# Turning the memory keys of four sequences on VectorE instead of TensorE

## The chip, the cores and the metric

One core of a Trainium2 chip runs the whole program in one launch. The metric is device time in microseconds (us), from the profiler's record of whole runs; a run is a little longer than its span, which goes from the first to the last instruction. TensorE (PE) multiplies matrices, and its weight loads (PEld) are recorded apart; VectorE (DVE) and ScalarE (ACT) work on rows of up to 128 partitions; GpSimd (POOL) does small work; SyncE (SP) issues most DMAs. Each engine runs its own instructions strictly in the order of the program and waits for semaphores of the others.

## The reference, cut to what matters

The program is one step of one decoder layer with width 1024. A prompt of 512 rows and a sample group of 8 sequences of 4 rows each go through the same weights: a mixer, cross-attention and a gated FFN. The change lies in the cross-attention, for the sample group:

```
def mem_attend(h, mk, mv, w_mq, w_mo):
    B, T, _ = h.shape
    q = (h @ w_mq).reshape(B, T, MEM_HEADS, MEM_HEAD_DIM)
    s = jnp.einsum('bqhd,bkhd->bhqk', q, mk) * (MEM_HEAD_DIM ** -0.5)
    p = jax.nn.softmax(s, axis=-1)
    o = jnp.einsum('bhqk,bkhd->bqhd', p, mv).reshape(B, T, D_MODEL)
    return o @ w_mo
```

There are 4 heads of 256. The prompt has one memory of 256 tokens. Each of the 8 sample sequences has 256 memory keys of its own, `cache_mem_k[b]` of 256 x 1024 in float32. The scores sum over the key's 256 head elements. In DRAM and in the SBUF stage the tokens lie on the partitions. A matmul sums over partitions, so the keys have to be turned before they can be an operand.

## The kernel before, in words

Weights and caches come by DMA into the pool `stg`: six stage buffers of 128 x 1024 float32. Weights are split into two fp32r halves (`split`, L146 on ACT and L147 on DVE) and go to the pool `wp`, four slots of 128 x 2 x 1024.

The query projection `h @ w_mq` is a `gemmB` (L465 and L477). Its output goes to `qh` and `ql` (high and low half for the prompt, L1348 and L1349) and to `qs` (the sample's queries, L1351). After it comes the attention, written as two interleaved parts.

The prompt's part is `prompt = pipe(8, ch_soft, idle, ch_turn, ch_out)`. One `next(prompt)` is one step: `ch_out` of item t-3, `ch_turn` of item t-2, `ch_soft` of item t, in that order. An item is one head with 256 rows. `ch_soft` has 12 score matmuls into `sca` (L1367), a maximum `cnm` on DVE (L1370), two exponentials on ACT (L1373), a reciprocal (L1374) and two scalings on DVE that write `cp` (L1376). `ch_turn` has four PE transposes into `cpt` (L1385), split into `pT` by ACT and DVE. `ch_out` has matmuls into `cpo` (L1397), split into `oT` by ACT and DVE.

The sample's part works on 16 chunks, two for each sequence, of 128 tokens x 1024. `mk_load` (L1407) brings a chunk into a stage buffer. `mk_turn` transposes it with eight PE transposes into `tpk` (L1416) in two groups of four, and each group is copied from PSUM to `kT`, in a slot of `wp` (L1417; the first group by ACT, the second by DVE). `mk_scores` (L1424) makes a sequence's scores `ssc` with eight matmuls, one for each head and half of its 256 elements; four of them lie side by side in TensorE's columns. Then come a maximum `snm` on DVE (L1035) and an exponential on ACT (L1036). Chunks 0 to 7 are turned during the query gemm; chunks 8 to 15, those of sequences 4 to 7, stand between the prompt's first steps. The values are then loaded by `mv_load` (L1428 and L1436) and summed in `mv_out` into `pso` (L1446).

What sets the order: the engines' programs are ordered by a scheduler from the order of the source; `tc.issue_after(x)` keeps what is written inside it behind instruction x, and `tc.high_priority()` moves work ahead. PSUM has two pools: five buffers (`mmp`: sca, ssc, cpo, pso and others) and three (`at`: tpk, cpt and others). Behind the attention stands the gemm with `w_mo`, and before it 24 small DMAs on SP's queue bring the convolution's rows into the tile `cr` (L1511 to L1513), which PE transposes later (`cvp`, L1525).

Of the kernel before, what the change touches and what calls it, by code (L numbers as in the profile page):

```python
# [7 lines left out]
F32 = mybir.dt.float32  # L8
F32R = mybir.dt.float32r
BF16 = mybir.dt.bfloat16  # L10
I32 = mybir.dt.int32
AF = mybir.ActivationFunctionType
ALU = mybir.AluOpType
AX = mybir.AxisListType

P = 128
DM = 1024
SEQ = 512
NB = 8
TS = 4  # L20
NS = NB * TS
ROWS = SEQ + NS
H = 4
# [54 lines left out]
def kernel(ctx: ExitStack, tc: tile.TileContext, I, O):  # L78
    nc = tc.nc
    MUL, ADD, SUB, MAX, MIN = ALU.mult, ALU.add, ALU.subtract, ALU.max, ALU.min  # L80
    NSLOT = 4
# [7 lines left out]

    cst = ctx.enter_context(tc.tile_pool(name="cst", bufs=1))  # L90
    sp = ctx.enter_context(tc.tile_pool(name="sp", bufs=11))
    wp = ctx.enter_context(tc.tile_pool(name="wp", bufs=NSLOT))
    stg = ctx.enter_context(tc.tile_pool(name="stg", bufs=6))
    npool = ctx.enter_context(tc.tile_pool(name="npool", bufs=5))
    t2p = ctx.enter_context(tc.tile_pool(name="t2p", bufs=8))
    zp = ctx.enter_context(tc.tile_pool(name="zp", bufs=3))
    sm = ctx.enter_context(tc.tile_pool(name="sm", bufs=4))
    psm = ctx.enter_context(tc.tile_pool(name="psm", bufs=5, space=bass.MemoryType.PSUM))
    psa = ctx.enter_context(tc.tile_pool(name="psa", bufs=3, space=bass.MemoryType.PSUM))
    dram = ctx.enter_context(tc.tile_pool(name="dram", bufs=1, space=bass.MemoryType.DRAM))  # L100

    def S(shape, dt, name):
        return sp.tile(list(shape), dt, name=name, tag="S")

    def N(name, w=1024):
        return npool.tile([P, 1032], F32, name=name, tag="N")[:, :w]
# [10 lines left out]
    def mmp(name="mm"):  # L117
        return psm.tile([P, 512], F32, name=name, tag="mm")
# [11 lines left out]
    mm = nc.tensor.matmul  # L130
# [4 lines left out]
    VRED = nc.vector.tensor_reduce  # L135
    VCP = nc.vector.tensor_copy
    GTT = nc.gpsimd.tensor_tensor
    ACT = nc.scalar.activation
    dma = nc.sync.dma_start
# [67 lines left out]
    W = Weights(NSLOT)  # L207
# [2 lines left out]
        return stg.tile([P, 1024], F32, name="wst", tag="st")  # L210

    def slot_tile():
        return wp.tile([P, 2, 1024], F32R, name="wslot", tag="W")

    def split_w(sv, st, share):

# [123 lines left out]
    @contextmanager  # L340
    def burst(ins):

        if ins is None:
            yield
        else:
            with tc.issue_after(ins), tc.high_priority():
                yield
# [227 lines left out]
    for i, _ in enumerate(mem_k()):  # L575
        if i in HSTEPS:
            j = HSTEPS.index(i)
# [53 lines left out]
    kT = S([P, H, ROWS], F32, "kT")  # L631
# [22 lines left out]
    for c0, c1 in HALF:  # L654
        n = c1 - c0
        ps = mmp()
# [3 lines left out]
        t = T2([64, n], "gt")  # L660
# [47 lines left out]
    ps = at("gtp")  # L708
# [3 lines left out]
    ps = at("gtp")  # L712
# [190 lines left out]
    ps = at("npt")  # L903
# [37 lines left out]
    ps = at("nT0")  # L941
# [34 lines left out]
    ps = at("nTt")  # L976
# [17 lines left out]
    r, ss = gq[:, 14:15], gq[:, 15:16]  # L994
# [177 lines left out]
    for b in range(4):  # L1172
        c = slice(b * P, b * P + P)
# [3 lines left out]
    kst, kts, pts, aTs, outs, rcs = {}, {}, {}, {}, {}, {}  # L1177
# [5 lines left out]
            gather("cache_dk", b, g, kst[b][g])  # L1183

    def dk_turn(b):
        kt = kts[b] = wp.tile([P, H, 260], F32, name="kT", tag="W")
        nc.gpsimd.tensor_copy(out=kt[:, :, 256:260], in_=dkT[:, :, SEQ + TS * b:SEQ + TS * (b + 1)])
        for g in range(2):
            ps = at("tpk")
            for h in range(H):  # L1190
                tr(ps[:, h * P:(h + 1) * P], kst[b][g][:, h * P:(h + 1) * P], ident)
            (VCP if g else nc.scalar.copy)(out=kt[:, :, g * P:(g + 1) * P], in_=v2(ps, P))
# [56 lines left out]
    prompt = pipe(4 * H, da_soft, lambda i: None, da_turn, da_av, da_end)  # L1249
    sall = S([P, NB, 260], F32, "das")  # L1250
# [85 lines left out]
    qs = sm.tile([P, 8, NS], F32, name="qs", tag="qz", bufs=1)  # L1336
    qh, ql = [], []

    def ev_q(m):
        if m % 2 == 0:  # L1340
            qh.append(npool.tile([P, 2, 516], F32R, name="qh", tag="N"))
        if m % 4 == 0:
            ql.append(S([P, 4, SEQ], F32R, "ql"))

        def ev(i, c0, c1, ps):
            n = min(c1, SEQ) - c0
            q = qh[m // 2][:, m % 2, c0:c0 + n]
            nc.scalar.mul(out=q, in_=ps[:, :n], mul=1.0 / 16.0)  # L1348
            STT(out=ql[m // 4][:, m % 4, c0:c0 + n], in0=ps[:, :n], scalar=1.0 / 16.0, in1=f32(q), op0=MUL, op1=SUB)  # L1349
            if i == 1:  # L1350
                nc.scalar.mul(out=qs[:, m, :], in_=ps[:, n:n + NS], mul=1.0 / 16.0)  # L1351
        return ev
# [3 lines left out]

    pTs, cps = {}, {}

    def ch_soft(i):
        h, bp = i // 2, i % 2  # L1360
        sv = v2(mmp("sca"), 256)
        for j in range(2):
            t0 = (2 * bp + j) * P
            for c in range(2):
                q, l = qh[h][:, c, t0:t0 + P], ql[h // 2][:, 2 * (h % 2) + c, t0:t0 + P]
                for m, (x, k) in enumerate(((q, 0), (q, 1), (l, 0))):
                    mm(sv[:, j, :], lhsT=x, rhs=mkT[k][:, 2 * h + c, :], start=(c + m == 0), stop=(c == 1 and m == 2))  # L1367
        nm = small(2, "cnm")
        su = small(2, "csu")
        VRED(out=nm, in_=sv, axis=AX.X, op=MAX, negate=True)  # L1370
        p = cps[i] = v2(Z("cp"), 256)
        for j in range(2):
            ACT(out=p[:, j, :], in_=sv[:, j, :], func=AF.Exp, bias=nm[:, j:j + 1], accum_out=su[:, j:j + 1])  # L1373
        nc.vector.reciprocal(out=su, in_=su)  # L1374
        for j in range(2):
            VTS(out=p[:, j, :], in0=p[:, j, :], scalar1=su[:, j:j + 1], scalar2=None, op0=MUL)  # L1376
# [27 lines left out]
    def mk_load(i):  # L1404
        b, c = i // 2, i % 2
        kst[i] = stage()
        dma(out=kst[i], in_=I["cache_mem_k"][0, b, c * P:(c + 1) * P].rearrange("t h d -> t (h d)"))  # L1407

    def mk_turn(i):
        b, c = i // 2, i % 2  # L1410
        if c == 0:
            kts[b] = wp.tile([P, 8, 256], F32, name="kT", tag="W")
        for q in range(2):
            ps = at("tpk")
            for j in range(4):
                t = tr(ps[:, j * P:(j + 1) * P], kst[i][:, (4 * q + j) * P:(4 * q + j + 1) * P], ident)  # L1416
            (VCP if q else nc.scalar.copy)(out=kts[b][:, 4 * q:4 * q + 4, c * P:(c + 1) * P], in_=v2(ps, P))  # L1417
        return t.ins

    def mk_scores(b):  # L1420
        ps = mmp("ssc")[:, :256]
        for c in range(2):
            for h in range(H):
                t = mm(ps[NS * h:NS * h + NS], lhsT=qs[:, 2 * h + c], rhs=kts[b][:, 2 * h + c, :], start=(c == 0), stop=(c == 1))  # L1424
        sample_exp(sall, b, ps, nm, su)
        return t.ins

    def mv_load(b):  # L1428

        if 2 < b < 7:  # L1430
            t = wp.tile([P, 2, DM], F32, name="vt", tag="W")
            vts[b] = [t[:, 0], t[:, 1]]
        else:
            vts[b] = [stage(), stage()]
        for c in range(2):
            dma(out=vts[b][c], in_=I["cache_mem_v"][0, b, c * P:(c + 1) * P].rearrange("t h d -> t (h d)"))  # L1436
# [18 lines left out]
    for i, _ in enumerate(gemmB(hqT, [ev_q(m) for m in range(4, 8)])):  # L1455
        if i % 4 == 3:
            for j in (i // 2 - 1, i // 2):
                mk_turn(j)
                mk_load(j + 6)

    next(prompt)
    for b in range(4):
        t = mk_scores(b)
    with tc.issue_after(t):
        for j in range(8, 16):
            t = mk_turn(j)
            if j + 6 < 2 * NB:
                mk_load(j + 6)
            if j == 11:
                next(prompt)  # L1470
    for b in range(3):
        mv_load(b)
    next(prompt)
    with tc.issue_after(t):
        for b in range(4, NB):
            t = mk_scores(b)
    for b in range(3, 7):
        mv_load(b)
    next(prompt)
# [24 lines left out]

    NUT = 43
    cvT = S([P, NUT, 20], F32, "cvT")
    conv0 = I["state_conv"][0].rearrange("b j c -> (b j) c")

    def conv_in(t, p0, o, c0, n):

        dma(out=t[p0:p0 + 16, o:o + n], in_=conv0[:, c0:c0 + n])  # L1511
        dma(out=t[p0 + 16:p0 + 19, o:o + n], in_=I["w_dw"][0][:, c0:c0 + n])
        dma(out=t[p0 + 19:p0 + 20, o:o + n], in_=I["b_dw"][:, c0:c0 + n])  # L1513


    cr = N("cr")
    for g in range(6):
        conv_in(cr, 20 * g, 0, 896 * g + (64 if g > 2 else 0), 896)
    conv_in(cr, 0, 896, 2688, 64)
    conv_in(cr, 0, 960, 5440, 64)  # L1520
    for t0 in (0, 4):
        ps = at("cvp")
        nt = min(4, 7 - t0)
# [356 lines left out]
```

## Time and profile before

| what | value |
|---|---|
| median of 3 runs | 957.77 us (955.96 to 959.61) |
| the profiled execution | 956.79 us |
| its span | 955.0 us |
| PE busy | 932.7 us, 98% of the span |
| DVE busy | 599.2 us, 63% |
| ACT busy | 388.8 us, 41% |
| mean granted TensorE clock | 0.993 |

The attention of the sample and the prompt lies between 441 and 500 us of the span. A view by lines gives, for each group, the line, the engine, the tiles (out<-in), the shapes, the count, the busy time, the mean duration of one in ns, and after the second bar the idle time before it with what ended it. Matmuls overlap, so a mean duration of theirs is longer than the distance from one start to the next.

### The profile page before, as it was taken

What the parts mean: (1) busy time and instruction counts of PE and PEld (TensorE: products, weight loads), DVE (VectorE), ACT (ScalarE), POOL (GpSimd) and SP (SyncE); (2) the same over time, 40 slices, a digit from 0 to 9 for tenths busy, and PEclk for the clock granted to TensorE, in tenths of its full rate; (3) what the DMA queues carried; (4) which work ended last, traced back from release to release, by engine and by line L of the source; (5) the groups of instructions that cost most, each with busy time, mean ns of one, the idle gap of its engine ahead of it and who ended that gap; (6) DMA issues with size and microseconds to landing.
All of it is one profiled execution on the core that took longest, in us unless ns stands there. A gap on an engine that the chain in (4) does not pass through costs nothing. (4 is left out here: it accounts for less than half of the span.)

```text
span 955.0 us, 17088 instructions
## 1 busy us (share of the span) xinstructions
PE 932.7 (98%) x6619; PEld 810.6 (85%) x6619; DVE 599.2 (63%) x1129; ACT 388.8 (41%) x750; POOL 197.5 (21%) x383
## 2 busy tenths in 40 slices
PE   8999999999999999999999999999999999999995
PEld 5899777879866778998777799989988997999974
DVE  5745144565887448635654769727758676676867
ACT  5655133344676447624544523332212222222232
POOL 6610000024432217300000444001110110111114
PEclk9999999999999999999999999999999999999998
DMA  8950023334825429955953743063053302512023
GB/s 278 309 184 2 1 89 136 89 110 150 264 90 183 155 94 329 307 155 167 353 213 114 206 134 89 4 177 89 4 144 79 122 26 79 165 48 89 24 92 116
DMA packets 120674, 130.27 MB, mean 136 GB/s; under 512 B 8568, under 2 KB 86233, under 8 KB 120593
## 3 DMA queue, kind: packets, MB, share of 16 engines
q1 hardware_dynamic: 114408, 125.69, 41.9%
q10 hardware_dynamic: 6184, 3.48, 1.2%
q8 instruction: 52, 0.85, 0.4%
q14 instruction: 30, 0.24, 0.1%
HBM read 112.22 MB, written 16.93 MB: 135 GB/s over the span
## 5 line engine op out<-in xcount | busy, mean ns | idle before, releaser
L146 ACT CAST wslot<-wst 128x1024 fp32r<-128x1024 f32 x125 | 130.9, 1050 | 259.9 <-issue 74.7
L477 PE MATMUL mm<-fT,wslot 128*128 128x256 f32 x1872 | 235.9, 288 | 0.0
L477 PEld LDWEIGHTS mm<-fT,wslot 128*128 128x128 f32 x1872 | 234.4, 188 | 1.8 <-issue 0.8
L147 DVE TENSOR_TENSOR wslot<-wst,wslot 128x1024 fp32r<-128x1024 f32 x125 | 155.1, 1245 | 89.3 <-ACT wslot L146 88.8
L1691 PE MATMUL mm<-wslot,act 128*128 128x512 f32 (+1 forms) x180 | 70.2, 391 | 0.0
L1692 PE MATMUL mm<-wslot,act 128*128 128x512 f32 (+1 forms) x180 | 70.0, 392 | 0.0
L1690 PE MATMUL mm<-wslot,act 128*128 128x512 f32 (+1 forms) x180 | 69.3, 387 | 0.0
L1598 POOL COPY cvo<-u 128x2 f32<-128x2 f32 x43 | 11.0, 256 | 204.8 <-DVE u L1596 194.7
L407 PE MATMUL mm<-wslot,hT 128*128 128x512 f32 x128 | 52.2, 408 | 0.0
L409 PE MATMUL mm<-wslot,hT 128*128 128x512 f32 x128 | 51.5, 403 | 0.0
L408 PE MATMUL mm<-wslot,hT 128*128 128x512 f32 x128 | 51.3, 401 | 0.0
L477 PE MATMUL mm<-hT,wslot 128*128 128x256 f32 (+1 forms) x384 | 51.0, 289 | 0.0
L1593 DVE TENSOR_TENSOR u<-mm,rsb 128x256 f32<-128x256 f32 x43 | 18.2, 424 | 51.0 <-PE mm L477 50.1
L477 PEld LDWEIGHTS mm<-hT,wslot 128*128 128x128 f32 x384 | 49.2, 188 | 0.5 <-issue 0.2
L1690 PEld LDWEIGHTS mm<-wslot,act 128*128 128x128 f32 x180 | 34.3, 191 | 8.0 <-issue 0.8
L1691 PEld LDWEIGHTS mm<-wslot,act 128*128 128x128 f32 x180 | 33.8, 188 | 7.2
L1692 PEld LDWEIGHTS mm<-wslot,act 128*128 128x128 f32 x180 | 33.8, 188 | 7.2 <-issue 0.4
L1610 ACT ACTIVATE c<-c 128x560 f32<-128x560 f32 x21 | 14.1, 672 | 56.7 <-DVE c L1604 56.7
L1604 DVE SCALAR_TENSOR_TENSOR c<-u,cvT,c 128x560 f32<-128x560 f32 x43 | 34.3, 798 | 0.9
L1603 DVE SCALAR_TENSOR_TENSOR c<-u,cvT,c 128x560 f32<-128x560 f32 x43 | 34.1, 793 | 0.2
L1703 DVE TENSOR_TENSOR yp<-mm,yp 128x512 f32<-128x512 f32 (+1 forms) x41 | 27.2, 674 | 5.1 <-PE mm L1692 5.0
L409 PEld LDWEIGHTS mm<-wslot,hT 128*128 128x128 f32 x128 | 24.5, 191 | 5.3
(474 smaller groups left out, 1857.7 us busy)
## 6 DMA issues: line engine op xcount, KB each, us to landing
wst<-in_w_up_dram SPq DMA_DIRECT2D x42, 512.0 KB
wst<-in_w_in_dram SPq DMA_DIRECT2D x28, 512.0 KB
wst<-in_w_down_dram SPq DMA_DIRECT2D x20, 512.0 KB
wst<-in_cache_mem_k_dram SPq DMA_DIRECT2D x16, 512.0 KB
wst<-in_w_mk_dram SPq DMA_DIRECT2D x8, 512.0 KB
xb<-in_x_prompt_dram SPq DMA_DIRECT2D x8, 512.0 KB
wst<-in_cache_dk_dram SPq DMA_DIRECT2D x16, 256.0 KB
wst<-in_cache_dv_dram SPq DMA_DIRECT2D x16, 256.0 KB
```

Of the source, the lines that this page charges most:

```text
L146: nc.scalar.copy(out=hi, in_=src)
L147: (eng or nc.vector).tensor_tensor(out=lo, in0=src, in1=f32(hi), op=SUB)
L407: mm(ps[b], lhsT=xt.hi(k, c0, c0 + n), rhs=s[:, 0, kk, :], start=(k == 0), stop=False)
L408: mm(ps[b], lhsT=xt.hi(k, c0, c0 + n), rhs=s[:, 1, kk, :], start=False, stop=False)
L409: return mm(ps[b], lhsT=xt.lo(k, c0, c0 + n), rhs=s[:, 0, kk, :], start=False, stop=(k == nk - 1))
L477: mm(ps[i], lhsT=s[:, l, k, :], rhs=x(k, c0, c1), start=(k == 0 and j == 0), stop=(k == 7 and j == 2))
L1603: STT(out=c, in0=u[:, 1:EXT - 1], scalar=w[1], in1=c, op0=MUL, op1=ADD)
L1604: STT(out=c, in0=u[:, 0:EXT - 2], scalar=w[0], in1=c, op0=MUL, op1=ADD)
L1690: mm(ps, lhsT=t[:, 0, c0:c0 + P], rhs=s[:, 0, i % 2, cs], start=st, stop=False)
L1691: mm(ps, lhsT=t[:, 0, c0:c0 + P], rhs=s[:, 1, i % 2, cs], start=False, stop=False)
L1692: return mm(ps, lhsT=t[:, 1, c0:c0 + P], rhs=s[:, 0, i % 2, cs], start=False, stop=en)
L1703: VTT(out=y, in0=ps, in1=y, op=ADD)
```

## The change

The keys of sequences 4 to 7 are no longer turned by PE. VectorE's stream transpose turns 32 x 32 blocks of a chunk from the stage buffer straight into one SBUF tile `kq` of 128 x 4 x 2 x 1024, one instruction per chunk and eight in all. The tile takes the place of the four weight slots: their pool is closed after the scores of sequence 3, the pool of `kq` is opened there, and the weight slots are opened again after the scores of sequences 4 to 7. The eight instructions stand in pairs between the prompt's steps, each held behind the latest `cnm` by `issue_after`.

With 32 x 32 blocks a key's elements lie on 32 partitions, so the scores (`kq_scores`) are 128 matmuls with 32 rows and 32 columns each, in 16 tiles of the array, into four PSUM tiles `ssq`. For the other operand the queries `qs` are written to DRAM (`qs_d`) and read back in four DMAs into `qrep`, where each group of 32 partitions has what it needs. Four copies (two on ACT, two on DVE) bring `ssq` into the order of tokens; one maximum on DVE and four exponentials on ACT follow.

The 24 DMAs of `cr` move from SP's queue to ACT's, into the query gemm.

```
-            kts[b] = wp.tile([P, 8, 256], F32, name="kT", tag="W")
+            kts[b] = slot([P, 8, 256], F32, "kT")
...
+    def kq_turn(i):
+        nc.vector.transpose(kq[:, i // 2 - 4, i % 2], kst[i])
+
+    def kq_scores(t):
+        ps = [mmp("ssq") for _ in range(4)]
+        kt = kq.rearrange("p b c (j r) -> p (b c) j r", r=NS)
+        for j in range(8):
+            for i in range(4):
+                r = slice(NS * i, NS * i + NS)
+                for h in range(H):
+                    with burst(t):
+                        t = mm(ps[i][NS * h:NS * h + NS, :256], lhsT=qrep[r, 2 * h + j // 4, j % 4, :], rhs=kt[r, :, 8 * h + j, :],
+                               start=(j == 0), stop=(j == 7)).ins
+        for i in range(4):
+            (VCP if i % 2 else nc.scalar.copy)(out=sall[:, 4:8, :].rearrange("p b (c i r) -> p b c i r", c=2, i=4)[:, :, :, i, :],
+                                               in_=ps[i][:, :256].rearrange("p (b c r) -> p b c r", c=2, r=NS))
+        VRED(out=nm[:, 4:8], in_=sall[:, 4:8, :], axis=AX.X, op=MAX, negate=True)
+        for b in range(4, 8):
+            ACT(out=sall[:, b, :], in_=sall[:, b, :], func=AF.Exp, bias=nm[:, b:b + 1], accum_out=su[:, b:b + 1])
...
+            conv_rows(i // 2 - 1)
+            conv_rows(i // 2)
 
     next(prompt)
     for b in range(4):
-        t = mk_scores(b)
-    with tc.issue_after(t):
-        for j in range(8, 16):
-            t = mk_turn(j)
-            if j + 6 < 2 * NB:
-                mk_load(j + 6)
-            if j == 11:
-                next(prompt)
+        with tc.issue_after(t):
+            mk_scores(b)
+    for key in list(lay)[::-1]:
+        closed(key)
+    opened("k", 1)
+    kq = lay["k"][1].tile([P, 4, 2, DM], F32, name="kq", tag="K")
+    dma(out=qs_d, in_=qs)
+    for j in range(8, 16):
+        with tc.issue_after(dve_last[0]):
+            kq_turn(j)
+        if j < 10:
+            mk_load(j + 6)
+        if j == 10:
+            for i in range(4):
+                dma(out=qrep[NS * i:NS * i + NS], in_=qs_d.rearrange("(j q) m n -> q m j n", q=NS))
+        if j in (9, 11, 13):
+            next(prompt)
     for b in range(3):
         mv_load(b)
     next(prompt)
-    with tc.issue_after(t):
-        for b in range(4, NB):
-            t = mk_scores(b)
+    kq_scores(pe_last[0])
+    closed("k")
+    opened("w", NSLOT)
+    slots_in("w")
```

VectorE's program before, from the scaling of the prompt's first item to that of its second (`kT<-tpk` are the copies of turned chunks):

```order
L1374 RECIPROCAL csu<-csu 128x2
L1035 TENSOR_REDUCE snm<-ssc 128x1
L1376 TENSOR_SCALAR cp<-cp,csu 128x256 x2
L1035 TENSOR_REDUCE snm<-ssc 128x1 x2
L1417 COPY kT<-tpk 128x4x128
L1370 TENSOR_REDUCE cnm<-sca 128x2
L147 TENSOR_TENSOR pT<-cpt,pT 128x256
L1417 COPY kT<-tpk 128x4x128
L1374 RECIPROCAL csu<-csu 128x2
L1376 TENSOR_SCALAR cp<-cp,csu 128x256
L1417 COPY kT<-tpk 128x4x128
L1376 TENSOR_SCALAR cp<-cp,csu 128x256
```

The same place in the program after, up to the scalings of the prompt's second and third item:

```order
L1055 TENSOR_REDUCE snm<-ssc 128x1 x3
L1458 STREAM_TRANSPOSE kq<-wst 128x1024 x2
L1402 TENSOR_REDUCE cnm<-sca 128x2
L1458 STREAM_TRANSPOSE kq<-wst 128x1024 x2
L167 TENSOR_TENSOR pT<-cpt,pT 128x256
L1402 TENSOR_REDUCE cnm<-sca 128x2
L1458 STREAM_TRANSPOSE kq<-wst 128x1024 x2
L1406 RECIPROCAL csu<-csu 128x2
L167 TENSOR_TENSOR pT<-cpt,pT 128x256
L1406 RECIPROCAL csu<-csu 128x2
L1408 TENSOR_SCALAR cp<-cp,csu 128x256 x4
L1402 TENSOR_REDUCE cnm<-sca 128x2
```

Six stream transposes now stand in VectorE's program ahead of the scaling that ends the prompt's second item; before, three copies of `tpk` stood there.

TensorE's program before, from the prompt's third item (`sca`) to its second turn (`cpt`):

```order
L1416 MATMUL tpk<-cpk,wst 128x128 x4
L1367 MATMUL sca<-mkT,ql 128x256
L1416 MATMUL tpk<-cpk,wst 128x128 x8
L1367 MATMUL sca<-mkT,qh 128x256 x2
L1367 MATMUL sca<-mkT,ql 128x256
L1367 MATMUL sca<-mkT,qh 128x256 x2
L1367 MATMUL sca<-mkT,ql 128x256
L1367 MATMUL sca<-mkT,qh 128x256 x2
L1367 MATMUL sca<-mkT,ql 128x256
L1416 MATMUL tpk<-cpk,wst 128x128 x40
L1424 MATMUL ssc<-kT,qs 32x256 x32
L1385 MATMUL cpt<-cpk,cp 128x128 x4
```

The same place after, from the end of the third item to the turn of the second:

```order
L1399 MATMUL sca<-mkT,qh 128x256 x2
L1399 MATMUL sca<-mkT,ql 128x256
L1417 MATMUL cpt<-cpk,cp 128x128
L1399 MATMUL sca<-mkT,qh 128x256 x2
L1399 MATMUL sca<-mkT,ql 128x256
L1399 MATMUL sca<-mkT,qh 128x256 x2
L1399 MATMUL sca<-mkT,ql 128x256
L1399 MATMUL sca<-mkT,qh 128x256 x2
L1399 MATMUL sca<-mkT,ql 128x256
L1399 MATMUL sca<-mkT,qh 128x256 x2
L1399 MATMUL sca<-mkT,ql 128x256
L1417 MATMUL cpt<-cpk,cp 128x128 x3
```

The transposes and the scores that stood between the third item and the second turn are gone, and the first matmul of that turn now stands directly behind the third item, ahead of the fourth.

## Rows read from the trace of the kernel before

**Rows 1.** The page: span, and busy time with its share of it.
```profile
span 955.0 us, 17088 instructions
PE 932.7 (98%) x6619; PEld 810.6 (85%) x6619; DVE 599.2 (63%) x1129; ACT 388.8 (41%) x750; POOL 197.5 (21%) x383
```

**Rows 2.** Busy time by stretch: length, each engine (count), PEclk, DMA share, GB/s.
```profile
441.00:450.00 9.00, 9.00 (x107) 6.64 (x106) 5.04 (x12) 4.87 (x16) 0.00 (x0) 1.00 0.54 171
450.00:460.00 10.00, 9.94 (x118) 7.99 (x120) 8.10 (x19) 6.31 (x19) 0.00 (x0) 1.00 0.88 290
470.00:480.00 10.00, 10.00 (x98) 7.87 (x96) 6.56 (x18) 5.92 (x21) 0.00 (x0) 1.00 0.84 324
480.00:490.00 10.00, 9.13 (x109) 6.33 (x108) 6.64 (x10) 6.46 (x12) 0.00 (x0) 1.00 0.98 349
```

**Rows 3.** Waits, 441 to 500 us: us in total, times, longest.
```profile
PEld pso L1446 <- DMA wst<-in_cache_mem_v_dram: 1.2, 1, 1.2
```

**Rows 4.** Timeline, 445.9 to 460.6 us: start, us, engine, line, operation, count.
```profile
445.96 1.53 PE L1416 MATMUL tpk<-cpk,wst 128*128 128x128 f32 x12
446.09 0.42 DVE L1035 TENSOR_REDUCE snm<-ssc 128x1 f32<-128x256 f32 x1 [0.44 <-PE ssc L1424]
447.25 0.48 PE L1367 MATMUL sca<-mkT,qh 128*128 128x256 f32 x2
448.74 0.60 PE L1385 MATMUL cpt<-cpk,cp 128*128 128x128 f32 x4
449.10 0.49 PE L1367 MATMUL sca<-mkT,qh 128*128 128x256 f32 x2
449.42 0.60 PE L1416 MATMUL tpk<-cpk,wst 128*128 128x128 f32 x4
450.77 0.48 PE L1367 MATMUL sca<-mkT,qh 128*128 128x256 f32 x2
451.92 5.09 PE L1416 MATMUL tpk<-cpk,wst 128*128 128x128 f32 x40
456.94 3.66 PE L1424 MATMUL ssc<-kT,qs 128*32 128x256 f32 x64
460.53 0.66 PE L1385 MATMUL cpt<-cpk,cp 128*128 128x128 f32 x4
```

**Rows 5.** DVE by line and form, 441 to 500 us.
```profile
L147 DVE TENSOR_TENSOR pT<-cpt,pT 128x256 fp32r<-128x256 f32 x16 | 6.6, 420 | 2.2 <-ACT pT L146 2.2
L1370 DVE TENSOR_REDUCE cnm<-sca 128x2 f32<-128x512 f32 x8 | 5.5, 689 | 3.3 <-PE sca L1367 3.2
L1376 DVE TENSOR_SCALAR cp<-cp,csu 128x256 f32<-128x256 f32 x16 | 5.1, 349 | 0.2
L147 DVE TENSOR_TENSOR wslot<-wst,wslot 128x1024 fp32r<-128x1024 f32 x4 | 4.9, 1226 | 2.6 <-ACT wslot L146 2.2
L1374 DVE RECIPROCAL csu<-csu 128x2 f32<-128x2 f32 x8 | 1.3, 162 | 2.6 <-ACT cp L1373 2.3
```

**Rows 6.** Instructions of line 318: ns (least/median/most), first and last start.
```profile
L318 DVE TENSOR_SCALAR hN<-xb,rs x5: 731/753/755, 21.6 to 47.8; 128x1024 f32<-128x1024 f32 x4, 32x1024 f32<-32x1024 f32 x1
```

**Rows 7.** Stretches with the granted clock, about 96 us and at the end.
```profile
96.10:99.50 3.40, 3.40 (x16) 2.28 (x15) 0.18 (x2) 0.00 (x0) 0.00 (x0) 0.50 0.00 0
943.80:946.00 2.20, 0.00 (x0) 0.00 (x0) 1.54 (x4) 0.00 (x0) 0.55 (x1) 1.00 0.31 119
946.00:955.00 9.00, 0.00 (x0) 0.00 (x0) 4.74 (x9) 2.14 (x7) 2.57 (x3) 0.50 0.32 117
```

**Rows 8.** ACT by line and form, 441 to 500 us, then its wait at line 1348.
```profile
L1373 ACT ACTIVATE cp<-sca,cnm 128x256 f32<-128x256 f32 x16 | 7.6, 483 | 4.3 <-DVE cnm L1370 4.2
L146 ACT CAST oT<-cpo 128x512 fp32r<-128x512 f32 x8 | 4.3, 590 | 7.3 <-PE cpo L1397 7.3
...
L1348 ACT ACTIVATE qh<-mm 128x256 fp32r<-128x256 f32 x9 | 3.0, 381 | 20.1 <-PE mm L477 20.1
```

**Rows 9.** Timeline: a DMA issue on ACT's queue; loads of the values on SP's.
```profile
49.89 0.42 ACTq L587 DMA_DIRECT2D masks<-in_consts_dram  x1
458.19 5.21 SPq L1436 DMA_DIRECT2D vt<-in_cache_mem_v_dram  x8
```

**Rows 10.** The page, DMA queue 10: packets, MB, share of 16 engines' span.
```profile
q10 hardware_dynamic: 6184, 3.48, 1.2%
```

More of the change, by code (lines that the diff above doesn't have):

```diff
@@ L91 @@
     sp = ctx.enter_context(tc.tile_pool(name="sp", bufs=11))
-    wp = ctx.enter_context(tc.tile_pool(name="wp", bufs=NSLOT))
     stg = ctx.enter_context(tc.tile_pool(name="stg", bufs=6))
@@ L97, with opened, closed, slots_in @@
     sm = ctx.enter_context(tc.tile_pool(name="sm", bufs=4))
+    lay, turns = {}, ["w"]
+    def opened(key, bufs):
+        c = tc.tile_pool(name=f"{key}{len(lay)}", bufs=bufs, side="right")
+        lay[key] = (c, c.__enter__())
+    def closed(key):
+        lay.pop(key)[0].__exit__(None, None, None)
+    def slots_in(*keys):
+        turns[:] = keys
+    def slot(shape, dt, name, key=None):
+        if key is None:
+            key = turns.pop(0)
+            turns.append(key)
+        return lay[key][1].tile(shape, dt, name=name, tag="W")
+    opened("w", NSLOT)
+    ctx.callback(lambda: [closed(key) for key in list(lay)[::-1]])
     psm = ctx.enter_context(tc.tile_pool(name="psm", bufs=5, space=bass.MemoryType.PSUM))
@@ L212, in slot_tile @@
     def slot_tile():
-        return wp.tile([P, 2, 1024], F32R, name="wslot", tag="W")
+        return slot([P, 2, 1024], F32R, "wslot")
     def split_w(sv, st, share):
@@ L1185, in dk_turn @@
     def dk_turn(b):
-        kt = kts[b] = wp.tile([P, H, 260], F32, name="kT", tag="W")
+        kt = kts[b] = slot([P, H, 260], F32, "kT")
         nc.gpsimd.tensor_copy(out=kt[:, :, 256:260], in_=dkT[:, :, SEQ + TS * b:SEQ + TS * (b + 1)])
@@ L1337, with conv_rows @@
     qh, ql = [], []
+    conv0 = I["state_conv"][0].rearrange("b j c -> (b j) c")
+    cr = N("cr")
+    def conv_rows(g):
+        p0, o, c0, n = (20 * g, 0, 896 * g + (64 if g > 2 else 0), 896) if g < 6 else (0, 896 + 64 * (g - 6), 2688 + 2752 * (g - 6), 64)
+        for q0, m, src in ((0, 16, conv0), (16, 3, I["w_dw"][0]), (19, 1, I["b_dw"])):
+            nc.scalar.dma_start(out=cr[p0 + q0:p0 + q0 + m, o:o + n], in_=src[:, c0:c0 + n])
     def ev_q(m):
@@ L1357 @@
     pTs, cps = {}, {}
+    pe_last, dve_last = [None], [None]
     def ch_soft(i):
@@ L1366, in ch_soft @@
                 for m, (x, k) in enumerate(((q, 0), (q, 1), (l, 0))):
-                    mm(sv[:, j, :], lhsT=x, rhs=mkT[k][:, 2 * h + c, :], start=(c + m == 0), stop=(c == 1 and m == 2))
+                    pe_last[0] = mm(sv[:, j, :], lhsT=x, rhs=mkT[k][:, 2 * h + c, :], start=(c + m == 0), stop=(c == 1 and m == 2)).ins
         nm = small(2, "cnm")
         su = small(2, "csu")
-        VRED(out=nm, in_=sv, axis=AX.X, op=MAX, negate=True)
+        dve_last[0] = VRED(out=nm, in_=sv, axis=AX.X, op=MAX, negate=True).ins
         p = cps[i] = v2(Z("cp"), 256)
@@ L1418, in mk_turn @@
         return t.ins
+    qrep = S([P, 8, 4, NS], F32, "qrep")
+    qs_d = dram.tile([P, 8, NS], F32, name="qs_d")
+    def kq_turn(i):
[16 more added lines that the diff above has]
+            ACT(out=sall[:, b, :], in_=sall[:, b, :], func=AF.Exp, bias=nm[:, b:b + 1], accum_out=su[:, b:b + 1])
     def mk_scores(b):
@@ L1430, in mv_load @@
         if 2 < b < 7:
-            t = wp.tile([P, 2, DM], F32, name="vt", tag="W")
+            t = slot([P, 2, DM], F32, "vt")
             vts[b] = [t[:, 0], t[:, 1]]
@@ L1457 @@
             for j in (i // 2 - 1, i // 2):
-                mk_turn(j)
+                t = mk_turn(j)
                 mk_load(j + 6)
+            conv_rows(i // 2 - 1)
+            conv_rows(i // 2)
     next(prompt)
     for b in range(4):
-        t = mk_scores(b)
-    with tc.issue_after(t):
-        for j in range(8, 16):
-            t = mk_turn(j)
-            if j + 6 < 2 * NB:
-                mk_load(j + 6)
-            if j == 11:
-                next(prompt)
+        with tc.issue_after(t):
[15 more added lines that the diff above has]
+            next(prompt)
     for b in range(3):
@@ L1473 @@
     next(prompt)
-    with tc.issue_after(t):
-        for b in range(4, NB):
-            t = mk_scores(b)
+    kq_scores(pe_last[0])
+    closed("k")
+    opened("w", NSLOT)
+    slots_in("w")
     for b in range(3, 7):
@@ L1506 @@
     cvT = S([P, NUT, 20], F32, "cvT")
[L1507 to L1520, printed above, removed]
     for t0 in (0, 4):
```

## The prediction, made before the changed kernel ran

> **What bounds the kernel now.** I read the page's busy shares first: PE is busy 98% of the span, DVE 63%, ACT 41% [rows 1]. Then the stretches of the stage that changes. From 441 to 480 us PE is full, at a granted clock of 1.00, and DVE is between 5.0 of 9 and 8.1 of 10 us [rows 2]. So the stage goes at PE's pace. The waits confirm it: the one that costs PE more than half a microsecond for data is the sum over the values, which waits 1.2 us for a transfer near 480 us [rows 3], which is the 0.9 us that PE lacks in the last stretch of [rows 2]. Work taken from PE here is therefore time, as long as nothing makes PE wait instead. Last the timeline of PE and DVE from 446 us, where the first of the moved transposes stand, because the prompt's steps are a chain from PE through DVE back to PE [rows 4].
>
> **What PE loses.** The 64 transposes of chunks 8 to 15. Between starts [rows 4]: 12 from 445.96 to 447.25 (1.3 us); 12 from 449.42 to 450.77, with one score matmul of about 0.12 us among them (1.2 us); 40 from 451.92 to 456.94 (5.0 us). Sum 7.5 us. With it go 16 copies from PSUM, eight on DVE and eight on ACT, neither of which bounds the stage before. The 1.2 us for the transfer [rows 3] I expect to go too: PE reaches that sum later than before, and SP has 24 fewer issues ahead of its loads; if it stays, the sum below is 1.2 us higher. Together 8.7 us, the most that this change can give.
>
> **What PE gets in return.** The 32 score matmuls of sequences 4 to 7 (64 records from 456.94 to 460.53, 3.6 us for 16 rounds of four tiles side by side, so 0.22 us a round [rows 4]) become 128 matmuls, 256 records. If 16 tiles of the array work together, that is again 16 rounds, 3.6 us, a difference of nothing. If only four do, 64 rounds, 14.4 us, 10.8 us more. No matmuls in several row groups at once are in these rows. I take the first, since the four column tiles that are in them do run together.
>
> **What DVE gets.** Eight stream transposes of 128x1024. The trace has none. From below: the one-source scaling of 128x1024 in SBUF takes 0.75 us [rows 6]. From above: twice the two-source operation of 128x1024, 2 x 1.23 = 2.45 us [rows 5]. Between: 128x256 takes 0.42 and 128x1024 takes 1.23 in the two-source form [rows 5], 1.05 ns an element and 0.15 us a start; that is the form that goes one element at a time, and I take it, less some 0.07 us by which neighbours overlap: T = 1.15 us a transpose.
>
> [...]
>
> **Where the transposes stand is what decides.** Six of them lie in DVE's program between the last maximum of sequences 0 to 3 and the scaling of the prompt's second item, and the first matmul of that item's turn now lies on PE directly behind the third item's scores. PE's queue is strict, so all that follows waits for that scaling. DVE: the last `snm` ends at 446.09 + 0.42 = 446.5 [rows 4]. Then six transposes, 6T = 6.9. Then two maxima (0.69 each), two splits of `pT` (0.42 each), two reciprocals (0.16 each) and the first scaling (0.35), 2.9 us by their durations, 2.6 with the same overlap [rows 5]; the scaling of the first item is behind already. The scaling ends at 446.5 + 6.9 + 2.6 = 456.0. PE: the prompt's second item starts 1.3 us sooner than before, at 445.96, where the 12 transposes stood. An item with the turn that follows it takes 449.10 - 447.25 = 1.85 us, an item alone 448.74 - 447.25 = 1.49 us, so PE is through at 449.3 [rows 4]. PE idles 456.0 - 449.3 = 6.7 us. In the kernel before there was no such wait, since the 40 transposes and the scores of four sequences stood on PE between the third item and that turn [rows 4].
>
> **Smaller waits.** The row tiles need four of the five PSUM buffers at once, while the prompt's `cpo` hold them until ACT and DVE have split them: cast 0.59, the cast and split of `pT` behind the turn, about 0.4 each; 1.4 us [rows 5, 8]. The last pair of transposes stands ahead of a split of `pT`: 0.3 us. Four exponentials stand on ACT ahead of casts that `cpo` waits for: at 0.48 each with 0.2 for the read behind it that is 2.7 us, most of it beside PE's work, and I leave 0.8 and 0.6 us in two places. Together 3.1 us; the bounds are 1 us (all but the buffers hidden) and 4.5 us.
>
> **The clock.** PE stopped at 943.8; the clock was 1.00 for the next 2.2 us and 0.50 from 946.0 on [rows 7]. [...] What that costs: at 96.1 the clock was at half for 3.4 us while PE was busy, a loss of 1.7 us of work [rows 7]. I take 1.7; the bounds are 0 and, for two such spells, 3.4.
>
> **Parts that I cost at nothing.** The 24 issues of `cr` on ACT: at 0.42 each [rows 9] 10 us, spread over the query gemm, where ACT waits 20.1 us for PE's output in nine places [rows 8]; without that cover some of the copies of turned chunks would be late, up to 2 us. The trip of the queries through DRAM: 4 x 1024 pieces of 128 B. Queue 10, the one with small pieces, took 1.2% of 16 engines' 955 us for 6184 packets [rows 10], 30 ns each, so 4096 packets are 7.6 us on 16 engines. They are read about 447 to 455, where the transfers' share is 0.54 to 0.88 [rows 2], and wanted some 12 us later; if the values' loads are pushed back by what is left, PE can lose up to 4 us. The weight slots come back only after the new scores, so the values of sequences 3 to 6, loaded from 458.2 to 463.4 before [rows 9], come 10 us later; they are wanted from 482 us on.
>
> **The sum.** 6.7 + 3.1 + 1.7 - 8.7 = +2.8 us. The profiled execution took 956.79 us, so it would be 959.6; it lies 1.0 below the median of 957.77, and against the median I forecast 960.5 us. As the sum depends on 6T, every 0.1 us in T is 0.6 us.
>
> **The rivals.**
>
> Fast transposes: at 0.75 us, as the one-source scaling [rows 6], 6T = 4.5, the wait is 4.3 us; -8.7 + 4.3 + 3.1 + 1.7 = +0.4, about 958, and without the clock 956.5. For: one source, both ends in SBUF. Against: a transpose isn't a plain stream. It stays within what can be told.
>
> Slow transposes, the case on the other side of no change: at 2.45 us, twice the row in [rows 5], 6T = 14.7, the wait is 14.5 us, the sum +10.6, 968.4 us. It decides from T = 1.5, where the sum passes +4.8. [...] Against: no row shows a DVE operation at that rate.
>
> Row tiles that don't run together: +10.8 on the sum, 971 us. For: the rows show column tiles alone. Against: different parts of the array are idle.
>
> No wait: the scaling isn't what the turn waits for, or DVE is ahead by more than the rows let me see; then PE keeps the gain, -8.7 + 3.1, and the smaller waits may shrink to 1: 950 to 952. For: the stage is PE's. Against: DVE has 6T + 2.6 us of work there and PE 3.3 us, and for these to be equal T would have to be 0.1 us.
>
> **How the numbers follow.** About 0.5%, 4.8 us, is what a measurement of this kernel can tell from no change. Forecast, T from 0.95 to 1.5: chance 0.52, of which 0.42 ends within the bound and 0.10 above it (a second spell of the lower clock, or transfers pushed back); its own range is 957.5 to 965. Fast transposes 0.16: 0.14 within, 0.02 faster. Slow transposes 0.17 and row tiles 0.05: slower. No wait 0.10: faster. So faster 0.12, same 0.56, slower 0.32. The range from 953 to 968.5 leaves out the case without a wait and the end of the two slow ones, about 0.19 together.
>
> **What would show it.** In the profile after: no `tpk` from 446 us on; eight stream transposes of 1.1 to 1.2 us each; PE idle 6 to 7 us in one piece at about 449, released by DVE's scaling `cp`; a granted clock of 0.50 behind it; the row tiles in about 3.6 us; the wait for the values gone. A PE idle time under 3 us there, or transposes over 1.5 us, proves the forecast wrong in one direction or the other; so do row tiles of 10 us and more, or a wait for transfers in the sum over the values.

## The result, and the profile after

The changed kernel takes 963.2 us (median of 5 runs, 961.07 to 963.9) against 957.77 us before: 5.4 us more, a ratio of 1.0049 with an interval of 1.0026 to 1.0072. Run once more beside other kernels it gave 1.0059 (1.0041 to 1.0077). Both intervals lie above 1, so the change costs time. It costs about the half per cent (4.8 us) that the prediction took for what can be told from no change: the medians lie 5.4 us apart, and the ratio estimated from all runs is 0.49% above 1. The forecast was 960.5 us, 2.8 more than before, in a range of 953 to 968.5.

What happens before the stage shifts a run by 2 us or so either way (the stage begins between 437.1 and 440.5 us in the thirteen traces), so I measure the stage itself: from the start of the first prompt score (`sca`) to the start of the last matmul of the gemm behind it (`mm<-wslot,oT`). These are the first and the last time in the views of the two tiles, before:

```profile
L1367 PE MATMUL sca<-mkT,qh x64: 274/282/369, 439.7 to 479.5; 128*128 128x256 f32 x64
L409 PE MATMUL mm<-wslot,oT x64: 387/393/496, 491.9 to 544.9; 128*128 128x512 f32 x64
```

and after:

```profile
L1399 PE MATMUL sca<-mkT,qh x64: 274/282/562, 439.4 to 481.6; 128*128 128x256 f32 x64
L429 PE MATMUL mm<-wslot,oT x64: 392/394/477, 499.3 to 551.0; 128*128 128x512 f32 x64
```

The stage took 544.9 - 439.7 = 105.2 us before and 111.6 after, 6.4 more; the whole span is 961.4 instead of 955.0 us, also 6.4 more. So in these two executions all of the loss lies in this stage. PE's busy time fell while the span grew [rows 1]:

```profile
span 961.4 us, 17326 instructions
PE 930.6 (97%) x6747; PEld 806.2 (84%) x6747; DVE 602.3 (63%) x1128; ACT 384.6 (40%) x744; POOL 196.4 (20%) x383
```

The waits between 441 and 505 us, those of PE and of its weight loads (us in total, times, longest); they answer to [rows 3]:

```profile
PE cpt L1417 <- DVE cp L1408: 6.1, 1, 6.1
PEld pso L1503 <- DMA wst<-in_cache_mem_v_dram: 2.3, 1, 2.3
PE pso L1503 <- DMA wst<-in_cache_mem_v_dram: 1.9, 1, 1.9
PE cpo L1429 <- ACT pT L166: 1.6, 3, 0.6
PE ssq L1468 <- issue: 0.8, 1, 0.8
PE ssq L1468 <- DVE oT L167: 0.5, 1, 0.5
```

One wait stands out: 6.1 us of PE for the scaling `cp`. VectorE's timeline shows why; it answers to the start of [rows 4]:

```profile
445.14 0.42 DVE L1055 TENSOR_REDUCE snm<-ssc 128x1 f32<-128x256 f32 x1 [0.44 <-PE ssc L1481]
445.48 2.36 DVE L1458 STREAM_TRANSPOSE kq<-wst 128x1024 f32<-128x1024 f32 x2
447.77 0.65 DVE L1402 TENSOR_REDUCE cnm<-sca 128x2 f32<-128x512 f32 x1
448.34 2.35 DVE L1458 STREAM_TRANSPOSE kq<-wst 128x1024 f32<-128x1024 f32 x2
...
451.52 2.35 DVE L1458 STREAM_TRANSPOSE kq<-wst 128x1024 f32<-128x1024 f32 x2
...
454.23 1.12 DVE L1408 TENSOR_SCALAR cp<-cp,csu 128x256 f32<-128x256 f32 x4
```

VectorE has no idle time from 445.5 to 455.3 us, and six of its eight transposes lie ahead of the scaling. PE's timeline in the same place, and at the row tiles (the 128 small score matmuls; each leaves two records, that is, two lines in the trace):

```profile
448.29 0.28 PE L1399 MATMUL sca<-mkT,ql 128*128 128x256 f32 x1
454.71 0.45 PE L1417 MATMUL cpt<-cpk,cp 128*128 128x128 f32 x1 [6.14 <-DVE cp L1408]
...
462.69 0.63 PE L1468 MATMUL ssq<-kq,qrep 32*32 32x256 f32 x8
463.25 1.20 PE L1429 MATMUL cpo<-pT,mvN 128*128 128x512 f32 x4
464.38 0.66 PE L1468 MATMUL ssq<-kq,qrep 32*32 32x256 f32 x16
465.50 4.28 PE L1468 MATMUL ssq<-kq,qrep 32*32 32x256 f32 x204 [0.46 <-DVE oT L167]
470.58 0.71 PE L1468 MATMUL ssq<-kq,qrep 32*32 32x256 f32 x28 [0.81 <-issue]
471.23 0.66 PE L1417 MATMUL cpt<-cpk,cp 128*128 128x128 f32 x4
```

And the granted clock (the column behind POOL) in stretches around the wait, as in [rows 7]:

```profile
444.00:448.50 4.50, 4.50 (x48) 3.75 (x40) 3.84 (x7) 2.11 (x8) 0.00 (x0) 1.00 0.97 174
448.50:450.80 2.30, 0.07 (x1) 0.00 (x0) 2.30 (x3) 0.98 (x4) 0.00 (x0) 1.00 0.98 257
450.80:454.70 3.90, 0.00 (x0) 0.02 (x1) 3.90 (x9) 1.39 (x5) 0.00 (x0) 0.50 1.03 394
454.70:457.70 3.00, 2.99 (x14) 3.00 (x15) 0.65 (x3) 0.00 (x0) 0.00 (x0) 0.51 0.93 354
457.70:460.00 2.30, 1.84 (x13) 1.39 (x12) 2.24 (x3) 1.58 (x6) 0.00 (x0) 1.00 0.65 228
```

PE stands still from 448.5; 2.3 us later the granted clock is 0.50, and it is 0.51 for the first 3.0 us of PE's work after the wait.

### The profile page after: what moved, and what is told of

Its sections match the earlier page's. It is cut to its first block, busy times and chain, and to the rows that moved or that the text cites. A ratio compares the mean times of both kernels' runs of the same rounds, so it can differ in the third digit from the quotient of the medians.

```text
span 961.4 us, 17326 instructions
## 1 busy us (share of the span) xinstructions
PE 930.6 (97%) x6747; PEld 806.2 (84%) x6747; DVE 602.3 (63%) x1128; ACT 384.6 (40%) x744; POOL 196.4 (20%) x383
## 4 chain that ended last, share of the span: by engine, by line
PE 86%; DVE 7%; ACT 2%; DMA 2%; issue 2%; POOL 1%; DVEq 0%; SPq 0%; ACTq 0%; POOLq 0%
PE mm L497 32%; PE mm L429 7%; PE mm L427 7%; PE mm L428 7%; PE mm L485 6%; PE mm L1745 4%; PE mm L1747 4%; PE mm L1746 4%; PE sda L1231 2%; PE mm L406 1%; DVE wslot L167 1%; PE oda L1257 1%; PE sdn L406 1%; DVE kq L1458 1%; PE tp L348 1%
```

## The experiments

"Stage" is the stretch defined above, from each run's own two rows: 105.2 us before, 111.6 after, and 111.1 in the second run of the changed kernel. Time is the median, and the ratio goes against runs of the kernel before on the same chip. The runs were made on several chips, so the ratios are the better measure across rows. (Two expectations give 105.3 us for the stage before.)

| run | median us | ratio (interval) | stage us |
|---|---|---|---|
| e1_scal | 960.67 | 1.0025 (1.0005 to 1.0044) | 107.2 |
| e2_half | 958.49 | 1.0010 (0.9988 to 1.0031) | 106.0 |
| e3_vord | 961.12 | 1.0030 (1.0008 to 1.0052) | 109.4 |
| e4_ssq2 | 970.78 | 1.0135 (1.0087 to 1.0183) | 117.5 |
| e5_late | 959.89 | 1.0020 (1.0006 to 1.0035) | 105.6 |
| e6_before_vord | 958.4 | 1.0005 (0.9982 to 1.0027) | 105.8 |
| e7_cr_on_sp | 964.8 | 1.0078 (1.0054 to 1.0102) | 110.4 |
| e8_singles | 961.68 | 1.0049 (1.0034 to 1.0063) | 108.9 |
| e9_half_columns | 963.3 | 1.0061 (1.0039 to 1.0082) | 110.7 |
| e10_changed_again | 963.27 | 1.0059 (1.0041 to 1.0077) | 111.1 |
| e11_later | 959.91 | 1.0024 (1.0005 to 1.0044) | 107.4 |

**Is it the length of the transposes?** Half of each chunk goes to another engine, the order stays.

```
-        nc.vector.transpose(kq[:, i // 2 - 4, i % 2], kst[i])
+        d = kq[:, i // 2 - 4, i % 2]
+        nc.vector.transpose(d[:, :512], kst[i][:, :512])
+        nc.gpsimd.tensor_copy(out=d[:, 512:], in_=kst[i][:, 512:])
```

> The changed kernel with VectorE turning only the first half of each chunk; GpSimd copies the other half unturned, so the scores of sequences 4 to 7 are not those of the reference. VectorE's order stays, each transpose is half as long. By my sum the wait at the second turn falls by five to six times 0.55 us, from 6.1 to about 3 us, the clock stays 1.00 or the spell at half ends before PE resumes, and the run is 3 to 5 us shorter than the changed kernel (ratio 0.999 to 1.002). If the wait had another cause than the length of the transposes, it stays at 6 us and the ratio at 1.005. If GpSimd's copies disturb VectorE, the transposes are longer than 0.6 us.

The two instructions in the view of the tile `kq`, and the wait in PE's timeline:

```profile
L1460 POOL COPY kq<-wst x8: 612/616/734, 445.2 to 453.4; 128x512 f32<-128x512 f32 x8
L1459 DVE STREAM_TRANSPOSE kq<-wst x8: 668/688/701, 445.5 to 454.5; 128x512 f32<-128x512 f32 x8
```

```profile
451.55 0.30 PE L1417 MATMUL cpt<-cpk,cp 128*128 128x128 f32 x1 [2.97 <-DVE cp L1408]
```

The wait fell from 6.14 to 2.97 us, the granted clock stayed at 1.00 (three score matmuls in 0.36 us behind the wait, against 0.64 in the changed kernel), and the run is 4.7 us shorter, the stage 5.6 us. The transposes took 0.69 us, which is 0.15 + 512 x 1.05 ns by the rate taken in the forecast, so nothing shows that the copies on GpSimd disturbed them.

**Is it their place?** Each pair is held behind the step's last scaling.

```
-        dve_last[0] = VRED(out=nm, in_=sv, axis=AX.X, op=MAX, negate=True).ins
+        VRED(out=nm, in_=sv, axis=AX.X, op=MAX, negate=True)
...
-            VTS(out=p[:, j, :], in0=p[:, j, :], scalar1=su[:, j:j + 1], scalar2=None, op0=MUL)
+            dve_last[0] = VTS(out=p[:, j, :], in0=p[:, j, :], scalar1=su[:, j:j + 1], scalar2=None, op0=MUL).ins
```

> The changed kernel with each pair of stream transposes held behind the last scaling of the prompt's step instead of its maximum; all the work is the same. Two transposes stand now ahead of the scaling that the second turn waits for, instead of six. If the place in VectorE's program makes the wait (my theory): the wait of 6.1 us at that turn shrinks to about 2 us, the granted clock stays 1.00 behind it (another 1.5 us), some of it comes back as waits of later steps, and the run is 2.5 to 4 us shorter than the changed kernel, ratio to the kernel before 1.000 to 1.003. If VectorE's total of nine more microseconds decides, wherever they stand: under 1 us shorter, ratio 1.004 to 1.006.

PE's waits in its timeline, with VectorE's last pair ahead of the second, and the clock from there on:

```profile
450.71 0.30 PE L1417 MATMUL cpt<-cpk,cp 128*128 128x128 f32 x1 [1.64 <-DVE cp L1408]
...
458.94 2.37 DVE L1458 STREAM_TRANSPOSE kq<-wst 128x1024 f32<-128x1024 f32 x2
461.41 6.97 PE L1468 MATMUL ssq<-kq,qrep 32*32 32x256 f32 x256 [2.50 <-issue]
```

```profile
458.90:461.40 2.50, 0.01 (x1) 0.02 (x1) 2.50 (x4) 1.57 (x6) 0.00 (x0) 1.00 0.96 351
461.40:463.40 2.00, 1.99 (x83) 1.39 (x91) 1.99 (x6) 0.00 (x0) 0.00 (x0) 0.94 0.86 262
463.40:466.80 3.40, 3.40 (x131) 2.97 (x103) 0.00 (x0) 0.00 (x0) 0.00 (x0) 0.53 0.40 149
```

The wait at the turn fell to 1.6 us, and the run by 2.5 us in its median, at the low end of my theory; the stage of the profiled execution fell by 4.4 us. Part of the 4.5 us came back at the row tiles: they now wait 2.5 us. The profile puts that down to "issue", but VectorE's last pair began at 458.94 and took 2.37 us, until 461.3, and PE starts at 461.4: by these times it is a wait for the keys. A spell of half clock comes here too, in the middle of the row tiles. So the place decides where PE waits, and a good part of VectorE's total is paid anyway.

**Can the rest be hidden by order alone?** Three orders on top of that one, in all of them sequence 7 summed last: the row tiles one prompt step later (e5_late), one prompt step ahead of each pair (e8_singles), the row tiles two steps later (e11_later).

```
     next(prompt)
+    next(prompt)
     kq_scores(pe_last[0])
```

> The run with the pairs behind the scalings, and two more moves of order: the row-tile scores one prompt step later, so that PE has a score step of 1.4 us and a turn ahead of them while VectorE ends its last pair, and the values of sequence 7 summed last. All the work is the same as in the changed kernel. If PE's waits for VectorE are what the change lost: the wait of 2.5 us ahead of the row tiles and the spell at half clock in them (1.7 us) go, the wait for the transfer falls to 1 us or less, and the run is 3 to 5 us shorter than the one with the pairs behind the scalings: 956 to 958 us, ratio 0.997 to 1.000. If the lost time only moves to the softmax of the sample, which now has less of PE's work ahead of its use: 960 us or more, with a wait at its matmuls.

Neither branch as it stands: the stage came to 105.6 us, 0.4 more than in the kernel before, but the median fell by 0.8 us only, with an interval that stays above 1. PE still waits 1.6 us at the turn, 1.2 us inside the row tiles, and these had another spell at half clock (granted 0.57 from 465.4 to 468.8). The 1.2 us, put to issue, come at the 25th record, the first that writes the fourth `ssq` tile. VectorE's split of `pT` out of `cpt` ends at 465.24 and PE goes on at 465.34, so by these times that tile waits for the buffer of `cpt`. (`cpt` lies in the pool of five, `mmp("cpt")`; the description of the kernel puts it into the other.)

```
-        if j in (9, 11, 13):
+        if j in (8, 10, 12, 14):
```

> The run with the late row tiles and sequence 7 last, and one prompt step more ahead of each pair: one stream transpose stands ahead of the scaling that the second turn waits for (six in the changed kernel, two in the run this is built on), one ahead of the third's, and the last stands alone ahead of the row tiles. Same work. If what is left of the loss are waits for VectorE: the wait of 1.6 us at the second turn falls under 0.8 us and the stage from the first score matmul to the last of the gemm behind it, 105.6 us there and 105.3 in the kernel before, falls to 104.5 to 105.3; ratio 0.998 to 1.001. If a transpose displaced is only waited for elsewhere: 105.5 us or more, ratio 1.002.

```profile
450.21 0.30 PE L1417 MATMUL cpt<-cpk,cp 128*128 128x128 f32 x1 [1.53 <-DVE cp L1408]
...
464.74 7.33 PE L1468 MATMUL ssq<-kq,qrep 32*32 32x256 f32 x256 [3.84 <-issue]
```

```profile
448.72 0.69 DVE L1402 TENSOR_REDUCE cnm<-sca 128x2 f32<-128x512 f32 x1 [0.52 <-PE sca L1399]
...
463.40 1.24 DVE L1458 STREAM_TRANSPOSE kq<-wst 128x1024 f32<-128x1024 f32 x1
```

This is the second branch: one transpose less ahead of the scaling saved 0.1 us, and the last transpose, which ends at 464.64, holds the row tiles for 3.8 us. The stage is 108.9 us. The 1.5 us that are left at the turn are not the transposes': VectorE stands idle for 0.5 us until PE has ended the third item's scores, and only then come the third item's maximum, a reciprocal, a split and, at 449.7, the scaling. By this trace the new order has a floor of about 1.5 us there, however fast a transpose is.

> The run with the pairs behind the scalings, sequence 7 last and late row tiles, with the row tiles one prompt step later still, so that VectorE has ended its last pair and split an output before PE comes to them. Same work. If the waits around the row tiles (1.2 us in them, and the spell at half clock over 3.4 us of them) are what keeps that run at 105.6 us for the stage: they go, the stage falls to 103 to 104 us against 105.3 in the kernel before, and the time to 955.5 to 957.5 us, ratio 0.998 to 1.000. If the sample's softmax, which has less of PE's work behind the row tiles, takes the time back: a wait of 1 us or more at its matmuls (spa) or at the first sum over the values (pso), and a ratio of 1.001 to 1.003.

Here the row tiles wait 0.4 us only and the clock stays at 1.00 (183 of their records in 3.93 us, 21 ns each), but the sample's softmax is late: PE waits 0.5 us at `spt` and 1.0 us (put to issue) at the first sum over the values, and the stage is 107.4 us. The time came back as the second branch said. None of these orders beats the kernel before.

**The wait for the values.** Sequence 7 is summed last, in the changed kernel and in the one before.

```
-for b in (2, 1, 0, 7, 6, 5, 4, 3) for c
+for b in (2, 1, 0, 6, 5, 4, 3, 7) for c
```

> The changed kernel with the values of sequence 7 summed last instead of fourth; the same work. Theory: the load of sequence 7 can start only when the first three sequences' sums have freed stage buffers, so its latency of about 6 us moves along with PE and the wait of 1.9 us comes whatever went before; with the 64 records of the other sums (3.6 us) ahead of it, that wait goes and the run is about 1.9 us shorter than the changed kernel (ratio 1.003). Rival: transfers are short of bandwidth there, so the wait turns up at the next weights, and the time stays (1.005).

2.1 us shorter (2.2 in the stage), about what was expected, but by another sum: the wait for the load fell from 1.9 to 1.0 us and did not go, one of the three waits for `pT` went (0.5 us), and the idle time ahead of the last 28 row-tile records was 0.65 us shorter, which the edit does not explain. The load itself was slower than the 6 us of the theory: 7.2 us from its issue at 485.87 to its sum at 493.11. What slows it is not shown, so the rival of short bandwidth is not out.

> The kernel before, with the values of sequence 7 summed last and nothing else changed. Its trace has a wait of 0.9 to 1.2 us for that load. If the load's latency against the work on PE behind its issue makes the wait: 0.5 to 1.0 us shorter, ratio 0.999. If the wait moves to the next weights: ratio 1.000.

No wait for that load is left in this trace, but one of 1.4 us for a cast of `pT` is new, and the time is the same. So taking away this wait alone gained nothing in the kernel before.

**The price of a pass of row tiles.** The loop over j runs over `list(range(8)) * 2`.

> The changed kernel with the 128 row-tile matmuls of the scores run twice over (the second pass adds the same products again, so those scores are doubled). This prices one pass by itself. If a record costs 17 to 21 ns, as the trace of the changed kernel shows, whatever tiles are free: the second pass adds 4.3 to 5.4 us, ratio 1.009 to 1.011. If 16 tiles really run together at 0.22 us a round and only the start was slow: 3.5 us, ratio 1.0085. If fetching instructions limits it: more than 6 us, with idle times put down to issue.

(The second pass starts its sums anew, so it writes the same scores over the first; they are not doubled, as the expectation has it.) The stage grew by 117.5 - 111.6 = 5.9 us, the median by 7.6 us in four runs. The row tiles in the timeline:

```profile
465.62 7.12 PE L1468 MATMUL ssq<-kq,qrep 32*32 32x256 f32 x332 [0.42 <-DVE oT L167]
473.45 2.75 PE L1468 MATMUL ssq<-kq,qrep 32*32 32x256 f32 x128 [0.71 <-issue]
476.91 0.71 PE L1468 MATMUL ssq<-kq,qrep 32*32 32x256 f32 x28 [0.71 <-issue]
```

332 records in 7.12 us are 21 ns each, as in the changed kernel (204 in 4.28 us). A pass costs 5.9 us, of which idle times put down to issue are part; they stand 128 records apart here.

> The changed kernel with the row-tile matmuls on 128 columns instead of 256, so only sequences 4 and 5 are scored and their scores stand for 6 and 7 as well; the copies behind are eight of half the size. Number and kind of PE's instructions stay. If the row tiles go at the rate at which PE issues records (17 ns each in the trace of the changed kernel): they take as long as before, about 5.7 us from the 25th record, and the run is within 1 us of the changed kernel. If they go at the array's rate of 256 columns in 0.22 us a round of 16: half of 3.5 us goes, the run is 1.5 to 2 us shorter.

```profile
465.44 2.87 PE L1468 MATMUL ssq<-kq,qrep 32*32 32x128 f32 x204 [0.56 <-DVE oT L167]
469.97 0.71 PE L1468 MATMUL ssq<-kq,qrep 32*32 32x128 f32 x28 [1.67 <-issue]
```

Neither branch: with half the columns a record takes 14 ns instead of 21, so neither the columns alone nor the records alone set the rate. The 204 records are 1.4 us shorter, but the idle time ahead of the last 28 is 1.4 us longer than in the changed kernel beside it (e10_changed_again), and behind it comes a second spell at half clock (granted 0.51 from 470.6 to 473.6, three score matmuls in 0.64 us). So the time of the run, as long as the changed kernel's, says nothing of the columns; the rate of the records does. That idle time was 0.81, 0.47, 0.16, 0.71, 0.37, 1.67 and 0.30 us in seven traces, always put to issue; what it waits for stays open.

**The small DMAs.** `cr` is loaded on SP's queue again.

> The changed kernel with the 24 small DMAs of the convolution back on SP's queue at their old place. By my costing at nothing for this part: within 0.5 us of the changed kernel, ratio 1.004 to 1.006, and SP's loads of keys up to some us later but not waited for. If the move to ScalarE's queue cost time in the query gemm: faster by 1 us or more (1.003). If it was what let the keys come in time: slower by 1 us or more, with waits for keys at the stream transposes.

The median is 1.6 us higher than the changed kernel's, with overlapping intervals (1.0054 to 1.0102 and 1.0026 to 1.0072), but its stage is 1.2 us shorter, not longer, and no stream transpose waits for a key. (The 20.1 us of ACT that the prediction read as nine waits are nine instructions and four waits; the cover is the same.) No gain or loss of this part is shown; it is inconclusive.

> The changed kernel itself once more, beside the two others on the same chip, since runs differ by some 2 us in what happens before the stage. Ratio to the kernel before 1.003 to 1.007; the wait of 6.1 us at the second turn and the spell at half clock behind it, as in its first trace. If the wait was an accident of the first trace: under 3 us.

The same wait of 6.14 us, the clock at 0.50 behind it (453.0 to 456.0, three score matmuls in 0.64 us) and a stage of 111.1 us: it was no accident.

## Why the prediction was right, and where its sizes were off

The direction, the main mechanism and the range held, but the loss is twice the forecast's 2.8 us, and one of its own signs of being wrong came, a wait for a transfer in the sum over the values; the row tiles took 6.1 us where it looked for 3.6. By its own steps, in us of PE's time in the stage:

| step | forecast | measured |
|---|---|---|
| transposes gone from PE | -7.5 | -7.5: no `tpk` is left from 446 us on |
| wait for the scaling | 6.7 | 6.1 |
| smaller waits | 3.1 | 2.5 (2.9 against 0.4 before) |
| lower clock behind the wait | 1.7 | 1.3 (2.81 us for 13 matmuls, against 1.56 in e2_half) |
| row tiles against `ssc` | 0 | 2.5 |
| wait for the values | -1.2 | +1.0 (1.9 against 0.9) |
| sum | +2.8 | +5.9; the stage grew by 6.4, so 0.5 is not accounted for |

**The wait** was read from order and rows together, and e2_half shows that it follows the length of the transposes (3.2 us less for six times 0.53), e1_scal that it follows their place. A transpose takes 1.21 us and a pair 2.36; the maximum behind the first pair starts 2.29 us after it, so T is 1.15 between starts, as forecast. So the rival of slow transposes (2.45) is out, and so is that of fast ones (0.75). The rate from which T was taken holds: 512 elements more take 1.214 - 0.688 = 0.53 us, 1.03 ns each, against 1.05 ns for the two-source form in [rows 5]. That this form goes one element at a time was my reading of that rate; the rows show the time of an element, not how many VectorE takes at once.

**The clock.** That a wait of 6.7 us brings the lower clock was my estimate, from 1.00 for 2.2 us and then 0.50 without PE's work at the end of the span [rows 7]. Both traces of the changed kernel show it behind the wait, at 0.50 to 0.51; 3.0 us of standstill in e2_half did not bring it. It cost less than half of the 3.0 us that PE worked at 0.51, the measure that I had forecast by: from the first transpose of that turn to its second, with 12 score matmuls between, PE took 2.81 us (454.71 to 457.52), against 1.56 us at 1.00 in e2_half (451.55 to 453.11), 1.25 us more.

**The smaller waits** are 1.6 for `pT`, 0.5 for `oT` and 0.8 put to issue. That the sum came near is partly luck: the wait for the buffers was 0.5 and not 1.4, and the last was not in the forecast.

**Row tiles** is a term of the sum that was mis-sized, by 2.5 us. I took 16 tiles at 0.22 us a round, because the four column tiles of before run at that. Between 462.69 and 471.23 the row tiles fill 7.4 us (the four `cpo` records take 1.1); without the 1.3 us of waits counted above that is 6.1, against 3.6 for the scores that they replace. They do run together, 21 ns a record instead of 56, but not at the 14 ns that 0.22 us a round would make, which e4_ssq2 confirms; what sets the 21 ns stays open.

**The wait for the values** is the step that failed: "The 1.2 us for the transfer I expect to go too: PE reaches that sum later than before". PE does reach it 11 us later, but the load of sequence 7 needs stage buffers that the first sums free, so it starts later by as much. The view of SP's issues (start, length, engine) has it 0.7 us behind the start of the first sum before and 0.8 us after, at 486.1 instead of 475.5:

```profile
475.49 0.81 SPq L1436 DMA_DIRECT2D wst<-in_cache_mem_v_dram  x2
```

```profile
486.11 1.49 SPq L1493 DMA_DIRECT2D wst<-in_cache_mem_v_dram  x2
...
492.70 1.07 PE L1503 MATMUL pso<-wst,caz 128*32 128x256 f32 x16 [1.85 <-DMA wst<-in_cache_mem_v_dram]
```

and PE waits until 492.7, 2.3 us by its weight loads. A wait for a transfer that PE itself sets off moves along with PE, so the 1.2 us did not go. That it grew comes from the load: 6.6 us from issue to sum, against 5.5 before (481.03 - 475.49); why it took longer is not shown.

**No wait**, the rival of a gain: it would need VectorE's work ahead of the scaling to fit into PE's 3.3 us. Even with one transpose there (e8_singles) 1.5 us are left, and those come from the third item's maximum standing ahead of the scaling, so no speed of the transposes gives this case. The prediction did not count that floor.

## What to carry to other kernels

Work taken from the engine that bounds a stage is worth its time only if the engine that takes it is free at that place in its own queue; a share of 63% over the span says nothing of ten microseconds in which it is the next link of the chain. Moving the displaced work within that queue moved the wait from the turn to the row tiles and then to the softmax, and at best the stage came within 0.4 us of the kernel before. Before counting a wait for a transfer as saved, ask what starts the transfer.

## What the runs showed of the hardware that I had not expected

- Spells at half clock came in the middle of work too: in the run with pairs behind the scalings 2 us after PE had resumed from a standstill of 2.5 us (0.53 for 3.4 us). With one more step ahead of each pair (e8_singles) the row tiles began in such a spell, behind 3.8 us of standstill: 110 records in 3.46 us at 0.53, 31 ns each, not twice the 21 ns of full clock. With half transposes PE stood still for 3.0 us and the clock stayed at 1.00 from 451.5 to 470, so the length of one standstill does not tell by itself whether a spell follows.
- Row tiles of 32 x 32: 21 ns a record at 256 columns and 14 ns at 128, against 56 ns for four column tiles at 256 (64 records in 3.6 us).
- VectorE's stream transpose of float32: 1.21 us for 128x1024, 0.69 us for 128x512.
